# Three merge-gate chunks as block products in a Griffin-style residual block, on one Trainium2 core

## The chip, the cores and the metric

The kernel runs on one core of a Trainium2 chip. The metric is the device time of one execution in microseconds; the time of a version is the median of its runs. PE is the matrix engine (TensorE), DVE the vector engine, ACT the scalar engine, POOL GpSimd and SP the engine that issues most DMAs. Products of PE land in PSUM, which has eight banks; a tile of 128 x 512 fp32 fills one.

## What is computed

One layer on 512 frames of 1024 features, fp32:

```python
xn = rmsnorm(x, norm_mix_g)
q, k, v, xr, gr, ga, gb = split(xn @ w_in)                 # seven blocks of 1024 columns
ya = chunked_band_attention(q, k, v, rel_table) @ w_attn_out
xc = causal_depthwise_conv(xr, conv_w, conv_b)
hr = rg_lru(xc, ...)                                        # gates r, i; a scan over the frames
yb = (hr * gelu(gr)) @ w_rnn_out
g_a, g_b = sigmoid(ga + b_a), sigmoid(gb + b_b)             # the merge gates
h = x + (g_a * ya + g_b * yb) @ w_o
h = h + (silu(hn @ Wg) * (hn @ Wu)) @ w_ffn_out             # hn = rmsnorm(h)
out = rmsnorm(h, final_norm_g)
```

## The kernel before

**Arithmetic.** Every fp32 operand of PE is split into a high part (ACT copies it into fp32r) and a low part (DVE subtracts), and each product is three matmuls: high by high, high by low, low by high (`mm3`, L74 to L78; `split`, L80 to L83).

**Chunks.** The weights come in chunks of 256 columns (two tiles of 128) by 1024 rows. Their order is the list `chunks` (`plan`, L96, and the loops behind it). `prefetch(n)` (L308) loads and splits chunks in that order up to number n; `weights(name, ahead)` (L336) does so for a chunk and `ahead` more. A load is two DMAs of 512 KB from SP into `raw` tiles (three buffers); the split goes into `whl` tiles (four buffers, two for a chunk). A plain chunk is two calls of `project` (L342): for each of the two column tiles 8 blocks of rows by 3 matmuls, 512 columns wide, so 48 matmuls.

**Block products.** From chunk 2 on the two FFN input projections use seven products of blocks in place of eight: `weight_sums` (L181) makes four sums of weight blocks on DVE and splits seven blocks; `block_product` (L362) runs seven `product`s of 4 x 3 matmuls, 256 columns wide, so 84 matmuls, and lets ACT copy partial results out of PSUM between them (`keep`, L369). The other side needs four sums of blocks of the activations, made once.

**Order of the first part.** Chunks in sets by j = 0, 2, 4, 6: `xr` (conv), `gr` (GELU), `ga` for j < 4, `gb`. `gates_of(j)` (L754) is the recurrence of two channel tiles: products `rg` on PE (L709), then a chain over ACT and DVE (L721 tanh, L728 tanh, L729 exp, L731, L735, L759 square root, L740, L741 scan, L742) and the split of its result into `rnn` (L746 on ACT, L747 on POOL). Merge gates are `gate(w, j)` (L778): a projection and a tanh into `za` or `zb`. Behind the sets come q and k of head pair 0 (L858), v of the first head group (L964) and the way out of the branch, `yb` (L967 to L972): eight projections whose inner dimension is all eight `rnn` tiles, each multiplied into its gate. `scores(0)` stands ahead of the seventh. Then comes attention in a PE order written by hand (L973).

**PSUM.** Tag `mm` has four banks, `s` and `t` two each (L71). The first column tiles of `xr0` and `gr0` are begun early and hold all four `mm` banks; `rg` of j takes two `s` banks, of j + 1 two `mm` banks (L755); the first two tiles of `ga` take `t` (L779).

**What sets the order.** The tile framework's planner orders each engine's instructions by a simulated timeline: among those whose inputs and buffers are ready it takes what stands first in the program. Inside `manual_schedule` blocks the named engines keep the program's order. One such block holds ACT and DVE for the first two tiles (L785 to L800):

```python
        g = [gelu_in(0, po[0])]
        xch.append(conv_out(1, xc[1]))
        g.append(gelu_in(1, po[1]))
        prefetch(index["gb0"] + 1)
        for c in range(2):
            gelu_out(g[c], po[c])
```

`gelu_in` is L691 and L692, `gelu_out` L696 (ACT) and L697 (DVE); L697 is the last reader of the PSUM tile of `gr0`.

Of the kernel before, what the change touches and what calls it, by code (L numbers as in the profile page):

```python
# [8 lines left out]
F32 = mybir.dt.float32  # L9
# [5 lines left out]
P = 128  # L15
D = 1024
S = 512
# [21 lines left out]
def block_kernel(ctx: ExitStack, tc: tile.TileContext, x, norm_mix_g, w_in, b_merge, rel_table,  # L39
# [51 lines left out]

    chunks = []
    index = {}
    strassen = [f"f{w}{j}" for j in range(2, FT, 2) for w in "gu"]

    def plan(name, *parts, rows=0, kts=KT):  # L96
        index[name] = len(chunks)
        chunks.append((name, parts, rows, kts))

    for j in range(0, KT, 2):  # L100
# [6 lines left out]
    def plan_qk(pr):  # L107
        plan(f"qk{pr}", cols(w_in, C_Q + pr * P, P), cols(w_in, C_K + pr * P, P))
# [48 lines left out]
    def load(name, k):  # L157
        _, parts, rows, kts = chunks[index[name]]
        wide = sum(width for *_, width in parts)
        n = min(4 * CW // wide, kts - k)  # L160
        at = rows + k * P
        pl, bufs = wp, 3
        if name in strassen and name[0] == "f":
            loads[0] += 1
            pl, bufs = (room[0], 1) if loads[0] % 4 == 0 and loads[0] > 4 else (wp, 3)
        raw = pl.tile([P, n, wide], F32, tag="raw", bufs=bufs, name=f"raw_{name}_{k}")
        to = 0
        for src, col, width in parts:
            sp.dma_start(out=raw[:, :, to:to + width],
                         in_=src[at:at + n * P, col:col + width].rearrange("(k p) e -> p k e", p=P))  # L170
            to += width
        raws[name, k] = raw

    slots, loads = [0], [0]
    barrier = ["wo1"]
    room = [None]

    begun = {}
    spare = [None]

    def weight_sums(name, ahead=False):  # L181

        def blocks_of():
            for k in (0, 4):
                if (name, k) not in raws:
                    load(name, k)
            r0, r1 = raws.pop((name, 0)), raws.pop((name, 4))
            return r0[:, :, 0:P], r0[:, :, P:CW], r1[:, :, 0:P], r1[:, :, P:CW]

        if name not in begun:  # L190
            a11, a21, a12, a22 = blocks_of()
            s21, s34 = (sums_room.tile([P, 2, 4, P], F32, tag=tag, bufs=1, name=f"{tag}_{name}")
                        for tag in ("s21", "s34"))
            s2, s1, s3, s4 = s21[:, 0], s21[:, 1], s34[:, 0], s34[:, 1]
            first_sum = dve.tensor_add(s1, a21, a22)
            if name == "fu2":

                tc.keep_in_program_order(first_sum)
            dve.tensor_sub(s2, s1, a11)
            dve.tensor_sub(s3, a11, a21)  # L200
            dve.tensor_sub(s4, a12, s2)
        if ahead:
            slots[0] += 1
            o = sums_room.tile([P, 2, 2, 4, P], F32R, tag="whl", bufs=1, name=f"whl_{name}_s2")
            split(o[:, :, 0], o[:, :, 1], s21[:])
            begun[name] = (s34, {"s2": o[:, 0], "s1": o[:, 1]})
            return
        sc = room[0]
        blocks_ = {}
        if name in begun:  # L210

            a11, a21, a12, a22 = blocks_of()
            s34, blocks_ = begun.pop(name)
            s1 = s2 = None
            s3, s4 = s34[:, 0], s34[:, 1]
        for group in ((("a11", a11), ("a12", a12)), (("s2", s2), ("s1", s1)), (("s3", s3), ("s4", s4)), (("a22", a22),)):
            if group[0][0] in blocks_:
                continue
            if name == "fg2" and group[0][0][0] == "a":

                for key, src in group:
                    o = spare[0].tile([P, 2, 4, P], F32R, tag="act", bufs=13, name=f"whl_{name}_{key}")
                    split(o[:, 0], o[:, 1], src)
                    blocks_[key] = o
                continue
            pl, tag, bufs = sc, "a22", 2
            if len(group) == 2:
                slots[0] += 1
                pl, tag, bufs = (sums_room, "whl", 1) if slots[0] % 5 == 1 else (wp, "whl", 4)
# [238 lines left out]
    _, xnT = features(xnp, "xn", "xnT")  # L468


    vc = cp.tile([P, NV], F32, name="vc")
# [267 lines left out]
    def rnn_scan(j, u, a, ti, g):  # L739
        dve.scalar_tensor_tensor(ti[:], ti[:], 0.5, u, ALU.mult, ALU.mult)  # L740
        dve.tensor_tensor_scan(u, a[:], ti[:], 0.0, ALU.mult, ALU.add)  # L741
        dve.scalar_tensor_tensor(u, u, 0.5, g[:], ALU.mult, ALU.mult)  # L742
# [3 lines left out]
        act.activation(o[:, 0], u, AF.Copy)  # L746
        pool.tensor_sub(o[:, 1], u, f(o[:, 0]))  # L747
        return o

    rnn = []  # L750
# [50 lines left out]
    for j in range(0, KT, 2):  # L801
        if j:
            for c in range(2):
                conv[j + c] = rnn_conv(j + c, tile_of(f"xr{j}", c, ahead=2))
        for c in range(2):
            if j:
                po = tile_of(f"gr{j}", c, "t")
                conv[j + c] += (rnn_gelu(j + c, po),)
        if j:
            gates_of(j)  # L810
        for w in range(j // 4, 2):
            for c in range(2):
                gate(w, j + c)
            if j == w == 0:
                gates_of(j)


    def blocks(ap):
        return ap.rearrange("p (b i) -> p b i", i=P)
# [35 lines left out]
            pool.tensor_copy(kl[other, e], kl[own, e])  # L855
        qk[pr] += [kh, kl]

    q_tile(0)  # L858
    k_tile(0)
    rw2_stack.close()  # L860
    rw_stack.close()
    aw2_stack, aw2 = opened("aw2", 2)
    aw_stack, aw = opened("aw", 2, "right")

# [102 lines left out]
    for j in range(KT):  # L967
        if j == 6:
            prob = scores(0)
        po = mm_tile(f"po_yb{j}")  # L970
        project(po, weights(f"yb{j - j % 2}"), j % 2, rnn)
        dve.scalar_tensor_tensor(zB[j], zB[j], 1.0, po[:], ALU.add, ALU.mult)  # L972
# [29 lines left out]

    hp = ctx.enter_context(pool_of("h", 1, "right"))

    sums_room = ctx.enter_context(pool_of("sums", 1, "right"))
# [112 lines left out]
    def split_act(i):  # L1118
        o = act2[i]

        if i == 0:
            hi = acp.tile([P, 2, S], F32R, tag="act", bufs=13, name=f"act_hi{i}")
        elif i < 3:
            hi = sums_room.tile([P, 2, S], F32R, tag=("s21", "s34")[i - 1], bufs=1, name=f"act_hi{i}")
        else:
            if i == 3:
                hi_room.append(sums_room.tile([P, 2, 2, S], F32R, tag="whl", bufs=1, name="act_hi34"))
# [232 lines left out]
```

## Time and profile before

| | |
|---|---|
| time, median of 3 runs | 867.3 us (867.19 to 867.31) |
| the profiled execution | 867.3 us, of which 865.5 us are its span, from first to last instruction |
| PE clock granted | 0.998 of full speed |
| PE, DVE, ACT, POOL busy | 99%, 69%, 58%, 11% of the span |

A row of the page or of a view names line, engine, operation and tiles (`out<-in`). In a timeline the first two numbers are start and duration in us, xN is a count, and the bracket is the idle time of that engine just before and what ended it. A view of stretches gives the busy time of each engine in each stretch, in brackets the instructions that reach into it. Matmuls overlap in time, so the time of a stream of them is read from their starts, not from single durations.

### The profile page before, as it was taken

The page shows a single profiled execution, that of the slowest core. Times are in us where ns is not written, and L with a number is a line of the kernel's source. Part 1 is how long each engine was busy: PE and PEld are TensorE (multiplying, and loading weights), DVE is VectorE, ACT ScalarE, POOL GpSimd, SP SyncE. Part 2 cuts the span into 40 slices and gives each one's busy share as a digit, 9 for nine tenths or more (in the row PEclk, how much of TensorE's full clock was granted, in tenths as well). Part 3 has the DMA queues.
Part 4 walks back from the last instruction along what each step waited for, and adds up shares of the span by engine and source line. Part 5 has one row for each costly group of instructions (what it writes and reads, how often), then busy time and mean ns, then how long its engine had stood idle before and what let it go on. Part 6 is the DMA issues. An engine that isn't in the chain of part 4 may idle for free.

```text
span 865.5 us, 13353 instructions
## 1 busy us (share of the span) xinstructions
PE 856.4 (99%) x5130; PEld 761.1 (88%) x5130; DVE 600.9 (69%) x950; ACT 498.1 (58%) x878; POOL 95.2 (11%) x161
## 2 busy tenths in 40 slices
PE   9999999999999999999999999999999999999997
PEld 6988888888889889898888889999999999888885
DVE  5666656573456585766556556988888888698885
ACT  6595747752356585767633357555555556545434
POOL 2412111120112132221200000000000001000000
PEclk9999999999999999999999999999999999999999
DMA  9133232433323332232223712424333332437542
GB/s 289 57 119 106 68 120 76 123 98 98 109 88 95 81 103 74 81 113 64 74 76 121 266 51 72 145 79 131 109 98 98 99 98 85 148 100 227 185 134 97
DMA packets 88767, 96.39 MB, mean 111 GB/s; under 512 B 5784, under 2 KB 74992, under 8 KB 88704
## 3 DMA queue, kind: packets, MB, share of 16 engines
q1 hardware_dynamic: 87072, 92.03, 34.3%
q10 hardware_dynamic: 1232, 2.95, 0.9%
q8 instruction: 40, 0.66, 0.3%
q0 software_dynamic: 400, 0.57, 0.2%
q14 instruction: 23, 0.19, 0.1%
HBM read 93.39 MB, written 2.14 MB: 110 GB/s over the span
## 4 chain that ended last, share of the span: by engine, by line
PE 97%; DVE 1%; ACT 1%; DMA 0%; issue 0%; ACTq 0%; DVEq 0%
PE po_out L76 2%; PE po_out L77 2%; PE po_out L78 2%; PE o L941 2%; PE p_fu L78 2%; PE p_fg L78 2%; PE p_fg L77 2%; PE p_fg L76 2%; PE p_fu L76 2%; PE p_fu L77 2%; PE pT L921 2%; PE po_v L76 2%; PE po_v L78 2%; PE po_v L77 2%; PE po_gb L76 2%; PE po_xr L77 2%
## 5 line engine op out<-in xcount | busy, mean ns | idle before, releaser
L910 POOL TENSOR_SCALAR p<-p,rl 128x128 f32<-128x128 f32 (+3 forms) x61 | 34.9, 590 | 135.7 <-DVE rl L906 135.4
L905 ACT ACTIVATE p<-p,m 128x128 f32<-128x128 f32 (+1 forms) x64 | 35.7, 560 | 11.0 <-DVE m L904 10.8
L76 PE MATMUL po_v<-whl_v,xnT 128*128 128x256 f32 x128 | 36.5, 285 | 0.0
L78 PE MATMUL po_v<-whl_v,xnT 128*128 128x256 f32 x128 | 36.2, 283 | 0.0
L77 PE MATMUL po_v<-whl_v,xnT 128*128 128x256 f32 x128 | 36.2, 283 | 0.0
L1131 POOL TENSOR_TENSOR act_lo<-act,act_hi 128x1024 fp32r<-128x1024 f32 x1 | 2.4, 2405 | 300.7 <-ACT act_hi L1130 300.7
L76 PE MATMUL po_out<-whl_fo,act_hi 128*128 128x512 f32 (+1 forms) x80 | 30.8, 385 | 0.5 <-ACT c_u L370 0.5
L78 PE MATMUL po_out<-whl_fo,act_lo 128*128 128x512 f32 (+1 forms) x80 | 30.7, 384 | 0.0
L77 PE MATMUL po_out<-whl_fo,act_hi 128*128 128x512 f32 (+1 forms) x80 | 30.7, 384 | 0.0
L904 DVE CUSTOM_DVE_ANT_0 p<-s,bias 128x128 f32<-128x128 f32 (+1 forms) x64 | 29.1, 483 | 1.0 <-PE s L896 1.0
L83 DVE TENSOR_TENSOR whl_qk<-raw_qk,whl_qk 128x1024 fp32r<-128x1024 f32 x16 | 20.5, 1284 | 13.2 <-ACT whl_qk L82 13.0
L83 DVE TENSOR_TENSOR whl_fu_s<-s_fu,whl_fu_s 128x1024 fp32r<-128x1024 f32 x20 | 24.1, 1222 | 6.2 <-ACT whl_fu_s L82 6.2
L77 PE MATMUL po_xr<-xnT,whl_xr 128*128 128x512 f32 (+1 forms) x80 | 27.7, 353 | 0.0
L83 DVE TENSOR_TENSOR pp<-pT,pp 128x384 fp32r<-128x384 f32 (+1 forms) x48 | 27.5, 596 | 0.1
L77 PE MATMUL po_gr<-xnT,whl_gr 128*128 128x512 f32 (+1 forms) x80 | 27.5, 347 | 0.0
L78 PE MATMUL po_gr<-xnT,whl_gr 128*128 128x512 f32 (+1 forms) x80 | 27.3, 347 | 0.0
L78 PE MATMUL po_xr<-xnT,whl_xr 128*128 128x512 f32 (+1 forms) x80 | 27.2, 346 | 0.0
L76 PE MATMUL po_gr<-xnT,whl_gr 128*128 128x512 f32 (+1 forms) x80 | 27.2, 347 | 0.0
L83 DVE TENSOR_TENSOR whl_fg_s<-s_fg,whl_fg_s 128x1024 fp32r<-128x1024 f32 x20 | 24.0, 1222 | 4.1 <-ACT whl_fg_s L82 4.0
L76 PE MATMUL po_xr<-xnT,whl_xr 128*128 128x512 f32 (+1 forms) x80 | 26.3, 351 | 0.4 <-ACT xnT L566 0.4
L82 ACT ACTIVATE whl_qk<-raw_qk 128x1024 fp32r<-128x1024 f32 x16 | 16.8, 1053 | 17.0 <-PE po_yb L78 10.4
L76 PE MATMUL po_gb<-xnT,whl_gb 128*128 128x512 f32 x64 | 25.2, 394 | 0.0
(487 smaller groups left out, 3247.5 us busy)
## 6 DMA issues: line engine op xcount, KB each, us to landing
raw_fg<-in_w_ffn_in_dram SPq DMA_DIRECT2D x24, 512.0 KB, 4.2
raw_fu<-in_w_ffn_in_dram SPq DMA_DIRECT2D x22, 512.0 KB, 3.9
raw_qk<-in_w_in_dram SPq DMA_DIRECT2D x32, 256.0 KB, 3.2
raw_fo<-in_w_ffn_out_dram SPq DMA_DIRECT2D x16, 512.0 KB, 3.6
raw_xr<-in_w_in_dram SPq DMA_DIRECT2D x8, 512.0 KB, 4.3
raw_gr<-in_w_in_dram SPq DMA_DIRECT2D x8, 512.0 KB, 3.6
raw_ga<-in_w_in_dram SPq DMA_DIRECT2D x8, 512.0 KB, 4.7
raw_gb<-in_w_in_dram SPq DMA_DIRECT2D x8, 512.0 KB, 3.5
```

What stands on the lines that cost most here:

```text
L76: pe.matmul(o, sh, mh, start=start, stop=False, skip_group_check=parts)
L77: pe.matmul(o, sh, ml, start=False, stop=False, skip_group_check=parts)
L78: pe.matmul(o, sl, mh, start=False, stop=stop, skip_group_check=parts)
L82: act.activation(hi, src, AF.Copy)
L83: dve.tensor_sub(lo, src, f(hi))
L904: dve.tensor_tensor_reduce(prob[qb][:], scs[qb][:, 0:w], bias[:, S - w:S], -1.0, 3e38, ALU.add, ALU.min, nmax[:, qb:qb + 1])
L905: act.activation(prob[qb][:], prob[qb][:], AF.Exp, bias=nmax[:, qb:qb + 1], scale=-1.0, accum_out=lsum[:, qb:qb + 1])
L910: eng.tensor_scalar(prob[qb][:], prob[qb][:], rl[:, qb:qb + 1], 1.0, ALU.mult, ALU.mult)
L921: pe.transpose(pt[:, at * P:(at + 1) * P], prob[qb][:, kb * P:(kb + 1) * P], ident[:])
L941: pe.matmul(po[:, S - n:S], st, pp[i][:, part, lo:lo + n], start=kb == 0 and part == 0, stop=kb == NT - 1 and part == 1)
L1131: (dve if i else pool).tensor_sub(lo[:], o[:], f(hi[:]))
```

## The change

- The chunk list gets a new order: xr0 gr0 ga0 **gb6** xr2 gr2 ga2 xr4 gr4 **qk0** xr6 gr6 **yb0 yb2 yb4 gb0 gb2 gb4 yb6 v0**, and then as before. So gb6 and ga0 stand behind the first pair, q and k of pair 0 between the third and the fourth set.
- gb0, gb2 and gb4 are computed as block products, with weight sums and four sums of blocks of `xnT`. Those sums are eight DVE operations of 1024 elements on each partition, four of them pinned behind the set j = 2, four behind the first GELU of the set j = 6. They lie in gate tiles that are not yet in use.
- Behind the recurrence: the splits of the four sums, the way out for yb0, yb2 and yb4 (ACT copies the result to `zb`), the three block gates (tanh, then one DVE operation that multiplies gate and way out), and the last two way-out tiles as before. Then `scores(0)`, and behind it v of the first group.
- The buffers for it are a new pool `gs`, where the recurrence's pool was.
- The low part of `rnn` 6 and 7 goes from POOL to DVE.
- The prefetch in the block quoted above goes one chunk further, up to xr2.

```diff
-    strassen = [f"f{w}{j}" for j in range(2, FT, 2) for w in "gu"]
+    strassen = ["gb0", "gb2", "gb4"] + [f"f{w}{j}" for j in range(2, FT, 2) for w in "gu"]
...
     for j in range(0, KT, 2):
         plan(f"xr{j}", cols(w_in, C_XR + j * P))
         plan(f"gr{j}", cols(w_in, C_GR + j * P))
         if j < 4:
             plan(f"ga{j}", cols(w_in, C_GA + j * P))
-        plan(f"gb{j}", cols(w_in, C_GB + j * P))
+        if j == 0:
+            plan("gb6", cols(w_in, C_GB + 6 * P))
+        if j == 4:
+            plan_qk(0)
...
-    plan_qk(0)
+    for name in ("yb0", "yb2", "yb4", "gb0", "gb2", "gb4", "yb6"):
+        plan(name, cols(*((w_in, C_GB + int(name[2]) * P) if name[0] == "g" else (w_rnn_out, int(name[2]) * P))))
     plan_v(0)
-    for j in range(0, KT, 2):
-        plan(f"yb{j}", cols(w_rnn_out, j * P))
...
-        pool.tensor_sub(o[:, 1], u, f(o[:, 0]))
+        (pool if j < 6 else dve).tensor_sub(o[:, 1], u, f(o[:, 0]))
...
-        prefetch(index["gb0"] + 1)
+        prefetch(index["xr2"] + 1)
...
+    def sums_of_x():
+        homes = [zs[w][j][:].rearrange("p a (b n) -> p (a b) n", n=256) for w, j in ((0, 2), (0, 3), (1, 2), (1, 1), (1, 0))]
+        x12, x22, t1, t2, t3 = homes
+        t4 = x12
+        todo = (lambda: dve.tensor_add(x12, f(block_of_x(0, 1, 0)), f(block_of_x(0, 1, 1))),
...
+        for n, what in enumerate(todo):
+            tc.keep_in_program_order(what())
+            if n == 3:
+                yield
+        yield t1, t2, t3, t4
+
+    for j in range(0, KT, 2):
+        if j:
+            for c in range(2):
+                conv[j + c] = rnn_conv(j + c, tile_of(f"xr{j}", c, ahead=2))
+            for c in range(2):
+                po = tile_of(f"gr{j}", c, "t")
+                conv[j + c] += (rnn_gelu(j + c, po),)
+                if j + c == 6:
+                    x_sums = next(sums_)
+            gates_of(j)
+        if j < 4:
+            for c in range(2):
+                gate(0, j + c)
+        elif j == 4:
+            q_tile(0)
+            k_tile(0)
+        if j == 0:
+            gates_of(0)
+            for c in range(2):
+                gate(1, 6 + c)
+        if j == 2:
+            sums_ = sums_of_x()
+            next(sums_)
...
+    def way_out(j):
+        for c in range(2):
+            po = mm_tile(f"po_yb{j + c}")
+            project(po, weights(f"yb{j}"), c, rnn)
+            act.activation(zB[j + c], po[:], AF.Copy)
+
+    def block_gate(j, n, x_right):
+        z, o = zs[0][2 + n % 2], zs[1][j // 2]
+        block_product(f"gb{j}", n % 2, x_right, z[:].rearrange("p a (b n) -> p (a b) n", n=256))
+        for c in range(2):
+            at = 24 + j + c
+            act.activation(z[:, c], z[:, c], AF.Tanh, bias=hb[:, at:at + 1], scale=0.5)
+        dve.scalar_tensor_tensor(o[:], z[:], 1.0, o[:], ALU.add, ALU.mult)
+
+    for i in (3, 2, 1, 4):
+        split_pair(bt_homes[i], x_sums[i - 1])
...
+    for j in (0, 2, 4):
+        way_out(j)
+    for n, j in enumerate((0, 2, 4)):
+        block_gate(j, n, x_right)
+
+    for j in (6, 7):
+        po = mm_tile(f"po_yb{j}")
+        project(po, weights("yb6"), j % 2, rnn)
+        dve.scalar_tensor_tensor(zB[j], zB[j], 1.0, po[:], ALU.add, ALU.mult)
...
-        po = mm_tile(f"po_v{gr}_{t}", "mm" if gr else "t")
+        po = mm_tile(f"po_v{gr}_{t}", "mm" if gr or t > 1 else "t")
...
+    prob = scores(0)
     for t in range(NT):
         v_tile(0, t)
```

More of the change, by code (lines that the diff above doesn't have):

```diff
@@ L162, in load @@
         pl, bufs = wp, 3
-        if name in strassen and name[0] == "f":
+        if name in strassen:
             loads[0] += 1
@@ L176, in block_kernel @@
     room = [None]
+    sums_room = [None]
     begun = {}
@@ L203, in weight_sums @@
             slots[0] += 1
-            o = sums_room.tile([P, 2, 2, 4, P], F32R, tag="whl", bufs=1, name=f"whl_{name}_s2")
+            o = sums_room[0].tile([P, 2, 2, 4, P], F32R, tag="whl", bufs=1, name=f"whl_{name}_s2")
             split(o[:, :, 0], o[:, :, 1], s21[:])
@@ L467, in block_kernel @@
     gm = cp.tile([P, 8], F32, name="gm")
-    _, xnT = features(xnp, "xn", "xnT")
+    xnT_all, xnT = features(xnp, "xn", "xnT")
     vc = cp.tile([P, NV], F32, name="vc")
@@ L800, in block_kernel @@
             conv[c] = xc[c], xch[c], g[c]
[L801 to L815, printed above, removed]
     def blocks(ap):
@@ L856, in k_tile, with block_of_x @@
         qk[pr] += [kh, kl]
-    q_tile(0)
-    k_tile(0)
+    def block_of_x(kh, half, part):
+        return xnT_all[:, 4 * kh:4 * kh + 4, part, half * 256:half * 256 + 256]
+    def sums_of_x():
[3 more added lines that the diff above has]
+        todo = (lambda: dve.tensor_add(x12, f(block_of_x(0, 1, 0)), f(block_of_x(0, 1, 1))),
+                lambda: dve.tensor_sub(t1, x12, f(block_of_x(0, 0, 0))),
+                lambda: dve.tensor_sub(t1, t1, f(block_of_x(0, 0, 1))),
+                lambda: dve.tensor_add(x22, f(block_of_x(1, 1, 0)), f(block_of_x(1, 1, 1))),
+                lambda: dve.tensor_sub(t2, x22, t1),
+                lambda: dve.tensor_sub(t3, x22, x12),
+                lambda: dve.tensor_sub(t4, f(block_of_x(1, 0, 0)), t2),
+                lambda: dve.tensor_add(t4, t4, f(block_of_x(1, 0, 1))))
+        for n, what in enumerate(todo):
[3 more added lines that the diff above has]
+        yield t1, t2, t3, t4
@@ L860, in block_kernel @@
     rw2_stack.close()
     rw_stack.close()
+    gs_stack, gs = opened("gs")
+    bt_homes = {i: gs.tile([P, 2, 4, 256], F32R, name=f"xt{i}") for i in (2, 1, 3, 4)}
+    sums_room[0] = room[0] = gs
+    def way_out(j):
[10 more added lines that the diff above has]
+        dve.scalar_tensor_tensor(o[:], z[:], 1.0, o[:], ALU.add, ALU.mult)
@@ new lines, in block_kernel @@
+    for i in (3, 2, 1, 4):
+        split_pair(bt_homes[i], x_sums[i - 1])
+    x_right = right_side(lambda kh, half, part, k: block_of_x(kh, half, part)[:, k], [bt_homes[i] for i in range(1, 5)])
+    for j in (0, 2, 4):
[6 more added lines that the diff above has]
+        dve.scalar_tensor_tensor(zB[j], zB[j], 1.0, po[:], ALU.add, ALU.mult)
@@ L862, in block_kernel @@
+    gs_stack.close()
     aw2_stack, aw2 = opened("aw2", 2)
@@ L962, in laid @@
                 3: ([qs(second)], [ks(second)])}[at]
+    prob = scores(0)
     for t in range(NT):
         v_tile(0, t)
[L967 to L972, printed above, removed]
     with tc.manual_schedule(engines={mybir.EngineType.PE}):
@@ L1003, in block_kernel @@
     hp = ctx.enter_context(pool_of("h", 1, "right"))
-    sums_room = ctx.enter_context(pool_of("sums", 1, "right"))
+    sums_room[0] = ctx.enter_context(pool_of("sums", 1, "right"))
+    slots[0] = loads[0] = 0
     hn_stack, hnp = opened("hnT", 1, "right")
```

12 lines of the change are left out of this document (6 added, 6 removed).

## The prediction

> **What bounds the kernel now.** I read the page first: the busy row and the chain that ended last.
>
> ```profile
> span 865.5 us, 13353 instructions
> PE 856.4 (99%) x5130; PEld 761.1 (88%) x5130; DVE 600.9 (69%) x950; ACT 498.1 (58%) x878; POOL 95.2 (11%) x161
> PE 97%; DVE 1%; ACT 1%; DMA 0%; issue 0%; ACTq 0%; DVEq 0%
> ```
>
> PE is busy 99% of the span and is 97% of the chain. Whether it is also without holes is told by the list of PE's waits, which has four rows:
>
> ```profile
> PE busy L396 <- DVE eps_t L402: 1.2, 1, 1.2
> PE pt_mix_0t L564 <- DVE xs_mix L544: 0.6, 2, 0.4
> PE po_out L76 <- ACT c_u L370: 0.5, 1, 0.5
> PE po_xr L76 <- ACT xnT L566: 0.4, 2, 0.2
> ```
>
> These are 2.7 us in all, and none lies between the first projections and the end of the FFN's input. So a change there wins only what it takes from the stream of matmuls, and loses every microsecond for which PE has nothing ready. For the price of the stream I took two stretches: one whole plain gate chunk (48 matmuls of 512 columns), and a piece of the FFN with block products alone (matmuls of 256 columns).
>
> ```profile
> core 0: us, PE busy (x), PEclk, DMA share, GB/s
> 94.57:105.45 10.88, 10.88 (x50) 1.00 0.32 97
> 570.00:670.80 100.80, 100.80 (x842) 1.00 0.34 105
> ```
>
> Two of the matmuls of each row only reach in over the edge. 10.88 / 48 is 0.2267 us for a wide matmul, 100.80 / 840 is 0.1200 us for a narrow one.
>
> **The saving.** A plain chunk costs 48 x 0.2267 = 10.88 us, a block chunk 84 x 0.1200 = 10.08 us. That is 0.80 us for a chunk and **2.40 us** for three. The numbers of matmuls are fixed by the code, and nothing else leaves PE: 864.9 us is the floor.
>
> [...]
>
> **What the block form asks of the other engines.** A block chunk adds on DVE four weight sums, the low parts of seven blocks, two additions from PSUM, and here one multiplication of 1024 elements; on ACT five copies out of PSUM. The FFN runs exactly this without a hole:
>
> ```profile
> core 0: us, PE busy (x) PEld busy (x) DVE busy (x) ACT busy (x) POOL busy (x), PEclk, DMA share, GB/s
> 560.00:740.00 180.00, 180.00 (x1503) 180.00 (x1502) 146.57 (x201) 107.16 (x191) 2.40 (x1) 1.00 0.34 105
> L1146 DVE TENSOR_TENSOR act<-act,c_u 128x1024 f32<-128x1024 f32 x9 | 11.0, 1219 | 0.3 <-ACT c_u L370 0.3
> ```
>
> DVE is 81% busy there and ACT 60%, so three such chunks in a row cost PE nothing once the first one's operands are there; without that cover a chunk's DVE work would take 146.57 / 180 x 10.08 = 8.2 us. The first operands have the three way-out chunks (32.6 us of PE) ahead of them. The eight sums of x are 1.22 us each (row above), 4.9 us in each batch. The first batch lies under the rest of set 2 and xr4. The second is pinned behind the GELU of tile 6, runs under the products of gr7, and ends near the end of the last gate products; the next 9 us of the chain there are nearly all ACT's. I cost both at nothing. The loads are as many and as large, on the same queue. Six way-out results are copied by ACT (0.63 us) where DVE multiplied (0.69 us); two low parts go from POOL to DVE. These shorten the chain or are neutral. `scores(0)` had 10.9 us of way-out tiles behind it and now has the 96 narrow matmuls of v, 11.5 us: nothing.
>
> **First new wait: the bank that gb6 needs (+2.5 us).** The prefetch in the hand-ordered block now takes in both splits of xr2, ahead of both `gelu_out`. Before, the planner put these splits between and behind them:
>
> ```profile
> 41.81 0.63 ACT L679 ACTIVATE xch<-xc 128x512 fp32r<-128x512 f32 x1 [4.47 <-DVE xc L675]
> 42.35 0.58 ACT L691 ACTIVATE g<-po_gr 128x512 f32<-128x512 f32 x1
> 42.83 2.00 ACT L82 ACTIVATE whl_gb<-raw_gb 128x1024 fp32r<-128x1024 f32 x2
> 44.72 0.62 ACT L696 ACTIVATE g<-g 128x512 f32<-128x512 f32 x1
> 48.64 1.06 ACT L82 ACTIVATE whl_xr<-raw_xr 128x1024 fp32r<-128x1024 f32 x1 [0.32 <-DMA raw_xr<-in_w_in_dram]
> 43.91 2.36 DVE L83 TENSOR_TENSOR whl_gb<-raw_gb,whl_gb 128x1024 fp32r<-128x1024 f32 x2 [0.26 <-ACT whl_gb L82]
> 46.19 0.68 DVE L697 SCALAR_TENSOR_TENSOR g<-g,po_gr 128x512 f32<-128x512 f32 x1
> 47.92 0.68 DVE L697 SCALAR_TENSOR_TENSOR g<-g,po_gr 128x512 f32<-128x512 f32 x1
> 49.73 1.23 DVE L83 TENSOR_TENSOR whl_xr<-raw_xr,whl_xr 128x1024 fp32r<-128x1024 f32 x1 [1.12 <-ACT whl_xr L82]
> 47.52 1.66 PE L709 MATMUL rg<-xch,wrg 64*128 64x512 f32 x12
> 49.11 0.50 PE L76 MATMUL po_gb<-xnT,whl_gb 128*128 128x512 f32 x1
> 18.74 18.91 SPq L169 DMA_DIRECT2D raw_gb<-in_w_in_dram  x2
> 39.52 6.01 SPq L169 DMA_DIRECT2D raw_xr<-in_w_in_dram  x2
> DMA to landing us min/median/max: 3.5/3.5/3.6
> ```
>
> First, the block's order is strict: ACT sat idle 4.47 us up to 41.81 although the gate chunk's first half was on its way since 18.74 and its split waited for none of what came in between. Second, the second half of xr2 cannot come sooner: its load goes out at 45.2 (the end of row 39.52, less 0.37 us of issue), when the first low part of the gate chunk has freed one of three raw buffers, and lands 3.5 us later, at 48.6. Now put that split ahead of `gelu_out`: high part until 49.7, low part until 50.96, then the first L697, which ends at 51.6 instead of 46.87. L697 is the last reader of a `gr0` tile. Of the four `mm` banks two hold the `gr0` tiles and two the gate products of tile 1, just finished; gb6 is next on PE at 49.11 and needs one of them. PE waits until 51.6: **2.5 us**. Behind it nothing is ready: xr2 needs the same banks, gr2's weights have not been loaded. Lower bound 0, if a bank comes free otherwise; upper bound 6.2, if the eight L721 (5.6 us) also go ahead of the tanh and the banks come with those, at 55.3. I take 2.5, where each term has its row.
>
> **Second new wait: the way out behind the recurrence (+1.0 us).** In the kernel before 35 us of gb6, q, k and v (163.34 to 198.34) stood between the last gate products and `yb`. Now `yb` follows at once, and each of its tiles needs `rnn` 6 and 7 for the last 6 of 24 matmuls. Four `mm` banks let PE do 4 x 18 x 0.2267 = 16.3 us ahead of them; that the planner does fill holes so is seen at 190.98, where seven `yb` matmuls stand between those of v. One block product of gb0 needs no `mm` bank (12 x 0.12 = 1.4 us), so the cover is 17.8 us. The chain before:
>
> ```profile
> 161.75 1.66 PE L709 MATMUL rg<-xch,wrg 64*128 64x512 f32 x12
> 163.34 0.50 PE L76 MATMUL po_gb<-xnT,whl_gb 128*128 128x512 f32 x1
> 171.59 0.66 ACT L780 ACTIVATE zb<-po_gb,hb 128x512 f32<-128x512 f32 x1
> 174.26 1.63 DVE L83 TENSOR_TENSOR whl_v<-raw_v,whl_v 128x1024 fp32r<-128x1024 f32 x1
> 175.13 1.05 ACT L82 ACTIVATE whl_v<-raw_v 128x1024 fp32r<-128x1024 f32 x1
> 176.20 1.28 ACT L759 ACT_TABLE_LOAD   x1
> 182.81 1.17 ACT L746 ACTIVATE rnn<-u 128x512 fp32r<-128x512 f32 x2 [2.23 <-DVE u L742]
> 190.98 0.40 PE L76 MATMUL po_yb<-rnn,whl_yb 128*128 128x512 f32 x1
> 198.34 0.40 PE L77 MATMUL po_yb<-rnn,whl_yb 128*128 128x512 f32 x1
> ```
>
> From 163.34 to the end of the first of the two copies (182.81 and half of 1.17) are 20.1 us. Of these 0.66 go with the gate that is no longer there, and the splits of v (1.63 and 1.05) were in the way too; without all three it is 16.8. Now the splits of yb and gb0 stand in their place, in part. I take 18.8 us, between, so PE waits **1.0 us**. Bounds: 0, and 3.8 (20.1 against 16.3 without the block product). The evictions behind it also wait for the split of the third sum of x, but 5.4 us of matmuls of the four open tiles remain, which cover ACT's 1.05, DVE's 1.22 and the copy.
>
> **The sum.** 867.3 - 2.4 + 2.5 + 1.0 = **868.4 us**. The profiled execution took 867.3 us (1.8 us outside the span), the same as the median.
>
> **The rivals.** I count as a difference what is over 0.2%, 1.73 us, about what a measurement of this kernel can tell from no change. So faster means stalls under 0.67 us in all, slower means over 4.13.
>
> Rival A, gb6 finds a bank: then 867.3 - 2.4 + 0 to 1.0, **864.9 to 865.9 us**. For it: in the kernel before the first L697 was over 2.2 us ahead of need, and the planner may sort gb6 ahead of tile 1's gate products. Against it: those products are ready first, and the four banks are counted out. Chance 0.24, of which 0.20 is under 865.57.
>
> Rival B, the recurrence is late: from 19.4 us after the gate products on (cover and 1.63 us), the way out alone pushes the sum over the bound; at 20.1 without the block product the time is 867.3 - 2.4 + 2.5 + 3.8 = **871.2 us**. For it: before it was 20.1, and both engines get more to do. Against it: the chain's own work is nearer 17. Chance 0.32.
>
> Rival C, narrow matmuls are slower in the new place: in the FFN the weight loads (PEld) are busy all 180 us, so nothing is left there; one load takes
>
> ```profile
> L76 PEld LDWEIGHTS po_ga<-xnT,whl_ga x16: 187/188/192, 36.0 to 46.5; 128*128 128x128 f32 x16
> ```
>
> 0.188 us, and were they not overlapped, three chunks would take 3 x (84 x 0.188 - 10.88) = 14.7 us more, **882 us**. Loads overlap wherever this trace has such products: chance 0.01. [...]
>
> The forecast itself has 0.43, from 867 to 869. So **faster 0.20**, **same 0.47** (0.43 and 0.04 of A), **slower 0.33**. The range 864.9 to 870.9 goes from the floor to nearly rival B's end and leaves out about one in ten.
>
> **What would show it.** Saving: three stretches of 84 narrow matmuls at 0.120 us ahead of attention, and wide ones unchanged. First wait: PE's list of waits gets a row for `po_gb` released by L697 on DVE, some 2.5 us near 49; if gb6 starts at 49.1, the step is wrong. Second wait: a row for `po_yb` released by `rnn`, 0 to 3.8 us, near 172 (163.34 less the chunk that has left, 10.9, and with the first wait, 2.5, and the cover). Block gates: no PE idle in them; waits for `keep` copies (L370) or `whl_gb` there would say that DVE or ACT is the bound. Wrong altogether would be a gain over 2.4 us, or stalls in attention or the FFN, whose code is as before.

## The result and the profile after

The changed kernel takes **875.56 us** (median of five, 874.20 to 876.00), the kernel before beside it 867.19 us: a ratio of 1.0091, 95% interval 1.0077 to 1.0106. It is slower by 8.4 us, where 1.1 us had been forecast. The profiled execution took 874.2 us.

The page of the changed kernel: span, busy row and chain.

```profile
span 872.4 us, 13641 instructions
PE 857.0 (98%) x5238; PEld 765.9 (88%) x5238; DVE 630.6 (72%) x988; ACT 515.3 (59%) x912; POOL 95.4 (11%) x159
PE 89%; DVE 4%; ACT 4%; DMA 1%; issue 1%; POOL 0%; ACTq 0%; DVEq 0%
```

DVE and ACT have 8% of the chain between them, where they had 2%: PE now waits for them. The list of PE's waits says where (the lines of the gates and the recurrence lie 3 further down, so L697 is L700, L721 is L724, L735 is L738, L746 is L749, L759 is L762):

```profile
PE po_yb L76 <- ACT rnn L749: 4.0, 1, 4.0
PE po_gb L76 <- DVE g L700: 2.7, 1, 2.7
```

These are the two rows that the prediction named, and the only new ones. The rest shows in the view of stretches, here of PE alone: length, busy time with matmuls, granted clock, DMA share, GB/s.

```profile
core 0: us, PE busy (x), PEclk, DMA share, GB/s
154.80:171.30 16.50, 16.50 (x74) 1.00 0.28 83
171.30:175.40 4.10, 0.17 (x1) 0.76 0.14 50
175.40:180.20 4.80, 4.73 (x11) 0.50 0.38 112
194.80:204.80 10.00, 10.00 (x85) 1.00 0.46 135
```

The first row is the way out ahead of the recurrence's last tiles: four banks, 16.4 us from first start to the end of the last. The second is the wait. The third was in no plan: **the granted clock is 0.50**, and 11 matmuls take 4.84 us from start to start, 0.43 us each after the first, in place of 11 x 0.2267 = 2.49. The fourth is a stretch of the block gates at 0.12 us a matmul, without a hole. (The list gives the second wait as 4.0 us; from the end of the matmul before, by the distance of the starts, to the next start are 4.1.)

The sum for the profiled execution: -2.4 (block form) + 2.7 (first wait) + 4.1 (second wait) + 2.3 (matmuls at half clock, 4.84 - 2.49) = 6.7 us, of the 6.9 us by which the span grew. The term of 2.3 us is what the matmuls lost there; the section on the prediction shows that a late copy would have cost as much at full clock. Three of the five executions took some 1.5 us more; the first experiment bears on that.

### The profile page after: what moved, and what is told of

Read it like the earlier page. It is cut to its first block, busy times and chain, and to the rows that moved or that the text cites. A ratio compares the mean times of both kernels' runs of the same rounds, so it can differ in the third digit from the quotient of the medians.

```text
span 872.4 us, 13641 instructions
## 1 busy us (share of the span) xinstructions
PE 857.0 (98%) x5238; PEld 765.9 (88%) x5238; DVE 630.6 (72%) x988; ACT 515.3 (59%) x912; POOL 95.4 (11%) x159
## 4 chain that ended last, share of the span: by engine, by line
PE 89%; DVE 4%; ACT 4%; DMA 1%; issue 1%; POOL 0%; ACTq 0%; DVEq 0%
PE po_out L76 2%; PE po_out L78 2%; PE po_out L77 2%; PE o L1008 2%; PE p_fu L78 2%; PE p_fg L78 2%; PE p_fg L77 2%; PE p_fg L76 2%; PE p_fu L76 2%; PE p_fu L77 2%; PE pT L988 2%; PE po_v L76 2%; PE po_v L78 2%; PE po_v L77 2%; PE po_ya L76 2%; PE po_h L76 2%
## 5 line engine op out<-in xcount | busy, mean ns | idle before, releaser
L76 PE MATMUL po_yb<-rnn,whl_yb 128*128 128x512 f32 x64 | 26.2, 418 | 4.0 <-ACT rnn L749 4.0
L83 DVE TENSOR_TENSOR whl_qk<-raw_qk,whl_qk 128x1024 fp32r<-128x1024 f32 x16 | 21.8, 1364 | 11.0 <-ACT whl_qk L82 10.7
L77 PE MATMUL po_yb<-rnn,whl_yb 128*128 128x512 f32 x64 | 25.6, 401 | 0.0
```

What stands on the lines that cost most here:

```text
L76: pe.matmul(o, sh, mh, start=start, stop=False, skip_group_check=parts)
L77: pe.matmul(o, sh, ml, start=False, stop=False, skip_group_check=parts)
L83: dve.tensor_sub(lo, src, f(hi))
```

## The experiments

Twelve kernels. Theory: the loss is the two waits, and what a wait does to PE's clock; the block form brings its 2.4 us. Rivals: a wait is not the prefetch's (or not the cover's) doing; the sums of x on DVE delay the recurrence; the half clock has another cause than the wait; the saving is not there.

**One line of the change alone.** The kernel before, with only the deeper prefetch:

```diff
-        prefetch(index["gb0"] + 1)
+        prefetch(index["xr2"] + 1)
```

> The kernel before with one line of the change alone: the prefetch in the hand-ordered block goes on to xr2. Theory (the split of xr2 ahead of both gelu_out holds a PSUM bank that the next gate chunk needs): PE waits 2.7 us for L697 near 49 us, as it does in the changed kernel, and the time is 867.2 + 2.7 = 869.9 us. Rival (that wait is made up later, by work that it lets come sooner, or stands only beside the other changes): 867.2 us.

871.30 us (869.71, 871.27, 871.32, 871.34), ratio 1.0043 (1.0028 to 1.0058). PE's longest wait in this kernel:

```profile
PE po_gb L76 <- DVE g L697: 2.6, 1, 2.6
```

and the stretch behind it, of PE alone:

```profile
51.60:55.00 3.40, 3.40 (x8) 0.50 0.49 157
```

The wait is the predicted one, in size and place (2.5 had been worked out). But three of four executions take 1.6 us more than that explains, and the profiled one of these has PE at half clock for 3.41 us behind the wait: 8 matmuls, where the changed kernel's profiled execution has 15 in the same 3.4 us at full clock. The mean granted clock of each execution sorts them alike: 0.999 in the run of 869.71, 0.997 in the three others.

**The pause filled.** The same kernel, with ten matmuls of 512 columns that nobody reads, between the gate products and gb6's place in the order (here gb0), in a spare bank:

```diff
+                for n in range(10):
+                    tc.keep_in_program_order(pe.matmul(warm_p[:], xnT[0][:, 0, 0:P], xnT[0][:, 0], start=True, stop=True))
```

> The kernel of b1_prefetch_further with ten matmuls of 512 that nobody reads put between the gate products of set 0 and those of gb0, in a spare bank: they fill 2.3 us of the 2.6 us in which TensorE waits for its first bank there. The chain of the bank is left as it was, so the wait's price of 2.5 us stays. If the half clock comes from TensorE's pause: no execution has the dip, all lie at 867.2 + 2.5 = 869.7 us, where b1 had 871.3 in three of four. Rival: the dip has another cause (the load of the other engines, a time of its own), it stays at 51.6 us or comes elsewhere, and the median stays at 871.3 us.

869.89 us (869.60 to 870.15, six runs), ratio 1.0031 (1.0019 to 1.0043). In this kernel the stretch of the wait and the one behind it read

```profile
48.00:51.60 3.60, 3.60 (x20) 1.00 0.87 286
51.60:55.00 3.40, 3.00 (x14) 1.00 0.58 170
```

The chain of the bank is as it was, and 0.4 us of the wait is left behind the fillers. The profile has no half clock, the mean clock of the six executions is 0.998 or 0.999, and all lie within 0.5 us of the one execution of the kernel above that had none. So the wait's own price is 2.8 us, and **the half clock is caused by PE's pause and costs 1.4 us more here**.

**The prefetch as it was.** The changed kernel with `prefetch(index["gb6"] + 1)` in the block.

> The changed kernel with the prefetch one chunk shorter, up to gb6. Theory: the wait of 2.7 us near 49 us goes and nothing else changes: 874.2 to 876.0 less 2.7, so 871.5 to 873.3 us; the wait for rnn and the half clock behind it stay. Rival (the prefetch of xr2 was needed elsewhere): as slow as the change, or slower.

871.53 us (871.47 to 871.71), ratio 1.0051 (1.0034 to 1.0067): 4.0 us less than the change. The first wait is gone, `po_yb` still waits 4.0 us, and the half clock behind it is as long (a mean clock of 0.75 from 168 to 175 us and of 0.77 from 175 to 182 make some 6.7 us of it; in the changed kernel it lasts from 173.44 to 180.27). As expected: the first wait and its clock are this one line's doing, and the rest of the loss lies at the recurrence.

**More cover behind the recurrence, by q and k.** The changed kernel, with q and k of pair 0 behind the gate products of set 6 in place of set 4, in the chunk list and in the loop.

```diff
-        if j == 4:
+        if j == 6:
             plan_qk(0)
...
-        elif j == 4:
+        elif j == 6:
             q_tile(0)
```

> The changed kernel with q and k of head pair 0 (10.9 us of PE) moved from behind set 4 to behind the gate products of set 6, so that they lie between these and the way out. Theory (PE runs out of work while the recurrence ends, and the 4.2 us without matmuls halve the clock for the matmuls behind): wait and half clock both go, 4.2 and 2.6 us: 874.2 - 6.8 = 867.4 us, and the runs lie closer together than 874.2 to 876.0. Rival (DVE and ACT are late with sums and splits whatever stands there): the wait moves behind q and k, and 2 us or more of it stay: over 869 us.

871.99 us (871.87 to 872.20), ratio 1.0055 (1.0040 to 1.0070). PE's two longest waits:

```profile
PE po_gb L76 <- DVE g L700: 2.8, 1, 2.8
PE po_yb L76 <- ACT rnn L749: 2.0, 1, 2.0
```

The rival's outcome came, over 869 us with 2.0 us of the wait left. PE has a chunk of 10.9 us more to do there, but the wait shrinks by 2.0 only. The view that groups ACT's instructions between 150 and 176 us shows a good part of why:

```profile
L841 ACT ACTIVATE kh<-po_k 64x512 fp32r<-64x512 f32 x2 | 1.2, 594 | 1.9 <-DVE kl L840 1.9
```

This and its like are q's and k's way out of PSUM (busy time, mean ns of one, idle time ahead of it and its cause); they hold ACT and DVE while the chain of the recurrence needs them. The first copy of `rnn` starts 24.5 us after the gate products, where it was 19.9 in the changed kernel. Of these 4.6 us, 1.3 lie ahead of the chain's first tanh, where nothing of q or k has run yet; from that tanh to the copy are 21.8 us in place of 18.5. Cover that needs the engines of the chain lengthens the chain. That they are late whatever stands there, the rival's reason, is what the cover by gb6 below refutes.

**Both.** The two edits above together.

> Both of the edits: prefetch one chunk shorter, q and k behind the gate products of set 6. Theory: only the saving of the block products is left, 867.2 - 2.4 = 864.8 us, up to 865.5 if moving q and k makes a small wait of its own. Rival (block products cost as much as plain ones here): 867.2 us or more.

869.10 us, ratio 1.0021 (1.0012 to 1.0031): one execution at 867.58 with a mean clock of 0.999, nine from 868.96 to 869.36 at 0.996 and 0.997. Missed by 3.6 us: the wait of 2.0 us stays, and in nine of ten executions the half clock comes with it.

**More cover, by gb6.** The changed kernel with gb6 behind the gate products of set 6, and q and k where the change has them.

```diff
-        if j == 0:
+        if j == 6:
             plan("gb6", cols(w_in, C_GB + 6 * P))
...
             gates_of(0)
+        if j == 6:
             for c in range(2):
                 gate(1, 6 + c)
```

> The changed kernel with the light chunk gb6 moved from behind the first pair to behind the gate products of set 6, ahead of the way out; q and k stay behind set 4, the prefetch line stays (xr2 is now the chunk behind ga0, so it loads as many chunks as the kernel before did). Theory: gb6 is 10.9 us of matmuls with one tanh a tile behind it, and unlike q and k it gives ACT and DVE little to do. Cover 10.9 + 16.3 = 27.2 us against some 20.6 us of recurrence, so the wait for rnn goes altogether; the bank wait near 49 us goes too, since xr2 stands where gb0 stood. Left is the saving: 867.1 - 2.4 = 864.7 us, runs close together. Rival (DVE and ACT are late whatever the cover, as with q and k): a wait for rnn of 1 us or more stays, 866 us or more. Rival 2 (with one light chunk less behind the first pair the chain of set 0 is late for set 2): a new wait between 50 and 110 us.

867.88 us, ratio 1.0009 (1.0000 to 1.0017). Both waits are gone: gb6 asks for one tanh a tile behind its products, the recurrence keeps its pace (its first copy of `rnn` ends 20.8 us after the gate products) and PE has 10.9 us more to do. A new wait stands where gb6 was taken away:

```profile
PE rg L712 <- ACT xch L682: 1.7, 1, 1.7
```

The timeline of DVE ahead of it, at 66 to 72 us:

```profile
66.29 2.77 DVE L744 TENSOR_TENSOR_SCAN u<-a,gt 128x512 f32<-128x512 f32 x2
...
70.83 0.73 DVE L678 SCALAR_TENSOR_TENSOR xc<-po_xr,vc,xc 128x509 f32<-128x509 f32 x1
```

The scans of set 0, which nobody needs soon, stand ahead of the conv's last tap, for which the gate products wait. Five executions lie at 867.06 to 867.40, five at 868.54 to 868.85, one between. The profiled one is of the slower five and has the half clock behind this wait; the mean clock of all five is 0.996, of the others 0.997 or 0.998. The second rival, a new wait between 50 and 110 us, came true.

**The scans later.** One more edit: the last three operations of set 0's recurrence (L743 to L745) are put behind the conv of set 2, and pinned there.

```diff
+        if j:
+            scans()
+
+    def scans():
         while held:
...
+            if j == 2:
+                scans()
```

> The kernel with gb6 as cover (867.1 to 868.9 us, one wait left: the gate products of set 2 wait 1.7 us for xch of tile 3, whose conv steps the planner put between the scans of set 0), with the last steps of the recurrence of set 0 (L740 of the kernel before and behind it) traced and pinned behind the conv of set 2. Theory: the conv of tile 3 ends some 4 us sooner, the wait goes, no pause of PE is left that could halve the clock, and only the saving is left: 867.1 - 2.4 = 864.7 us, 865.2 at most, with runs within 0.3 us. Rival (the scans, put off, are late for someone else): a new wait, 866 us or more.

**865.59 us**, ratio 0.9984 (0.9974 to 0.9993): faster than the kernel before (ten of eleven executions from 865.41 to 866.15; one took 1714.3 us and is left out). That is 0.4 us over the 865.2 that had been allowed. One new wait is left, and in the profile no half clock from the first projections to the end of the matmuls (mean clock 0.999):

```profile
PE rg L712 <- POOL xch L683: 0.6, 1, 0.6
```

A stretch of 10 us out of its block gates, PE alone:

```profile
190.00:200.00 10.00, 10.00 (x85) 1.00 0.35 122
```

**The saving by itself.** The last kernel, with gb0, gb2 and gb4 as plain chunks; the sums of x and their splits are still made, though nothing reads them.

```diff
-        block_product(f"gb{j}", n % 2, x_right, z[:].rearrange("p a (b n) -> p (a b) n", n=256))
...
+            po = tile_of(f"gb{j}", c)
+            act.activation(z[:, c], po[:], AF.Tanh, bias=hb[:, at:at + 1], scale=0.5)
```

> The same kernel with gb0, gb2 and gb4 at the same place as plain products (48 wide matmuls for a chunk), the sums of x and their splits kept though nobody reads them: what the block form alone is worth. Theory: 3 x (10.88 - 10.08) = 2.4 us slower than the one with block products, 867.1 us, as the kernel before. Rival (block products save less in this place, by waits for copies out of PSUM or for weight sums): under 1.5 us of difference.

868.03 us (867.84 to 868.23), beside the 865.59 on the same chip: the block form is worth **2.44 us**, 2.40 had been worked out. (The 867.1 that had been expected was missed because the kernel with block products itself lies 0.9 us over its forecast.) The same stretch holds 46 wide matmuls here, where the row above has 85 narrow ones:

```profile
190.00:200.00 10.00, 10.00 (x46) 1.00 0.34 107
```

**The last 0.6 us.** The low part of the conv's tile 7 on DVE in place of POOL.

```diff
-        pool.tensor_sub(xch[:, 1], xc[:], f(xch[:, 0]))
+        (dve if j == 7 else pool).tensor_sub(xch[:, 1], xc[:], f(xch[:, 0]))
```

> The kernel of e9_scans_later with one more edit: the low part of xch tile 7 is made on VectorE and not on GpSimd. In e9 TensorE waits 0.6 us at 140.8 us for that low part. If GpSimd is the late one: the wait is gone, 865.6 - 0.6 = 865.0 us. Rival: VectorE is as late there, the wait stays or moves to VectorE's name, 865.6 us or more.

865.62 us (ten of eleven runs from 865.48 to 865.81), ratio 0.9984 (0.9975 to 0.9993): nothing won. The wait at 140.8 us is gone, but another has come, as the rival had it in part:

```profile
PE po_yb L76 <- ACT rnn L751: 0.4, 1, 0.4
```

The recurrence ends no sooner: the first copy of `rnn` starts at 163.92 us, 163.82 in the kernel before this edit, and PE begins the matmuls that need it at 164.60 and 164.54. So the wait of 0.6 us had been hidden by this later limit, and the cover by gb6 is just long enough.

**The clock kept up at the second pause.** The kernel with the old prefetch, with 16 matmuls that nobody reads in the second wait, and the high-part products of `rnn` 6 and 7 of four tiles ahead of their low-part products.

```diff
+    for n in range(16):
+        tc.keep_in_program_order(pe.matmul(warm_p[:], pos[0][1](0, 0, slice(0, P)), rnn[0][:, 0], start=True, stop=True))
```

> The changed kernel with the shorter prefetch (871.5 us), and 16 matmuls of 512 columns into a spare bank, whose result nobody reads, pinned between the last way-out matmul that can run and the first that needs rnn 6; the products with the low parts of rnn are traced behind those with the high parts. Theory (of the 6.8 us lost there 4.2 are the wait and 2.4 to 2.6 the half clock that follows a pause of PE): the wait is filled with 3.6 us of useless work, the clock stays at 1.0, and 2.4 to 2.6 us come back: 869.0 us, with the way out as late as before. Rival (the matmuls behind the wait are slow for another reason, the low parts of rnn or the operands' place): 871.5 us, and matmuls at 0.43 us again.

871.30 us (870.45, 870.58, 872.01, 872.16), ratio 1.0048 (1.0034 to 1.0061). The two lower ones, one of them profiled, have a mean clock of 0.998, and the profile has no half clock; the others have 0.996. So with a full clock this kernel takes 870.5 us, 1.0 less than the 871.5 of the kernel with the old prefetch, where 869.0 had been expected. In the profile other waits take the place of the slow matmuls:

```profile
PE q_gb L76 <- ACT whl_gb_a L82: 1.1, 1, 1.1
PE po_yb L76 <- ACT zb L937: 0.5, 1, 0.5
```

The first is for the weights of the block gate, the second for a bank that ACT has not yet copied out. And the 1.0 us is not the clock's. The edit also moved a split of yb on DVE away from between the two L738, and the first copy of `rnn` starts at 171.06 us, 172.10 in the kernel with the old prefetch. From that copy to the first matmul of the fifth way-out tile are 9.05 us here at full clock (180.11) and 9.02 there with the half clock (181.12). So at the second pause the half clock costs nothing on top. (What makes the two upper executions 1.6 us slower is not shown: neither was profiled.)

**The sums of x earlier.** The kernel with the old prefetch, and all eight sums behind set 2.

```diff
-                if j + c == 6:
-                    x_sums = next(sums_)
...
             next(sums_)
+            x_sums = next(sums_)
```

> The changed kernel with the shorter prefetch (871.5 us) and all eight sums of x behind set 2, none behind the GELU of tile 6. If the second batch of sums (4.9 us of DVE between 2 us before and 6 us after the last gate products) makes the chain late, rnn 6 comes 1 to 2 us sooner and the time is 869.5 to 870.5. Theory (the chain's first 9 us there are ACT's, so the sums lie beside it): rnn 6 comes within 0.4 us of where it came, 871.1 to 871.6 us.

872.07 us (871.94 to 872.20), ratio 1.0057 (1.0043 to 1.0070). It is 0.5 us slower than with the sums where the change has them, and the wait for `rnn` is 4.4 us in place of 4.0. That is 0.5 us over the range that had been given for no effect, and slower, not 1 to 2 us faster: the sums do not make the recurrence late.

**The low parts on POOL.** The kernel with the old prefetch, and the low parts of `rnn` 6 and 7 back on POOL.

```diff
-        (pool if j < 6 else dve).tensor_sub(o[:, 1], u, f(o[:, 0]))
+        pool.tensor_sub(o[:, 1], u, f(o[:, 0]))
```

> The changed kernel with the shorter prefetch (871.5 us) and the low parts of rnn 6 and 7 on POOL again. Theory: the high parts set the end of the wait, and 16 matmuls need only these; a low part on POOL is 1.3 us in place of 0.65 but need not wait for the splits on DVE: the same within 0.4 us, 871.1 to 871.9. Rival (the low parts are what the way out waits for): 1 us slower or more.

875.62 us (875.51 to 875.70), ratio 1.0098 (1.0082 to 1.0113): 4.1 us slower than with them on DVE, where the same within 0.4 us had been expected; the rival was right. Behind the old wait stands a second one, and a third for the bank:

```profile
PE po_yb L76 <- ACT rnn L749: 4.0, 1, 4.0
PE po_yb L77 <- POOL rnn L750: 2.7, 1, 2.7
PE po_yb L76 <- ACT zb L903: 1.2, 1, 1.2
```

So that part of the change is needed.

## Why the prediction was wrong

**Saving, right.** 2.40 us worked out, 2.44 measured by doing and not doing it. The block gates run without PE idle time, so their sums, low parts and copies cost PE nothing while they run, as said; what is made for them ahead of that does, as the second failed step shows.

**First new wait, right in mechanism and size, short of its consequence.** The row is there, 2.7 us for 2.5, and the timeline of the changed kernel has the steps as they were worked out (ACT's lines first, then DVE's):

```profile
48.48 1.06 ACT L82 ACTIVATE whl_xr<-raw_xr 128x1024 fp32r<-128x1024 f32 x1 [2.43 <-DMA raw_xr<-in_w_in_dram]
49.44 1.13 ACT L699 ACTIVATE g<-g 128x512 f32<-128x512 f32 x2
...
49.56 1.23 DVE L83 TENSOR_TENSOR whl_xr<-raw_xr,whl_xr 128x1024 fp32r<-128x1024 f32 x1 [2.47 <-ACT whl_xr L82]
50.71 1.27 DVE L700 SCALAR_TENSOR_TENSOR g<-g,po_gr 128x512 f32<-128x512 f32 x2
```

The split of the second half ends at 50.8, the first L700 half of 1.27 later, and gb6 starts at 51.53. What the sum lacked is that PE then runs at half clock in most executions, 1.4 us more (in three of four of the kernel with this line alone; by their times in three of five of the changed one). Rival A (a bank comes free) is refuted.

**Second new wait: the failed step.** The prediction put it at 1.0 us, "cover" 17.8 against a chain of 18.8. It was 4.1. Both terms were off, as the timeline of the changed kernel shows (ACT's lines, then DVE's):

```profile
155.32 1.05 ACT L82 ACTIVATE whl_yb<-raw_yb 128x1024 fp32r<-128x1024 f32 x1
156.27 5.62 ACT L724 ACTIVATE gt<-rg,hb 64x512 f32<-64x512 f32 x8
169.48 1.06 ACT L762 ACTIVATE u<-u 128x1024 f32<-128x1024 f32 x1 [1.84 <-DVE u L738]
174.79 1.17 ACT L749 ACTIVATE rnn<-u 128x512 fp32r<-128x512 f32 x2 [3.30 <-DVE u L745]
...
167.63 1.21 DVE L83 TENSOR_TENSOR whl_yb<-raw_yb,whl_yb 128x1024 fp32r<-128x1024 f32 x1
168.76 0.68 DVE L738 SCALAR_TENSOR_TENSOR u<-u 128x512 f32<-128x512 f32 x1
```

The chain took 20.5 us, from 154.86 (the end of the gate products) to the end of the first `rnn` copy (174.79 and half of 1.17). The splits of yb took the places of the ones that had gone, in full and not "in part": one on ACT ahead of the eight tanh, one on DVE between the two L738 for which the square root waits (where this split is moved away, in the kernel that keeps the clock up, the copy of `rnn` comes 1.0 us sooner). The prediction had all rows for 20.1 and took 18.8 on the hope that some of it would go. And the block product of gb0 that was to lengthen the cover by 1.4 us did not come: its weights' first high part is made at 181.53 (a row of `whl_gb_a` below), 10 us too late. So the cover was 16.4 us, and 20.5 - 16.4 = 4.1. Rival B had this mechanism and nearly this size (3.8), at a chance of 0.32.

**The second failed step: the evictions behind it.** The prediction let 5.4 us of matmuls of the four open tiles cover the way out of the first bank, and put the step at nothing. In the changed kernel ACT waits 1.77 us for the low part of `rnn` (L750) and copies that bank out only after the splits of the sums and three of gb0's splits, which it makes without idle time between them; the last line is PE's first matmul of the fifth tile, which needs the bank:

```profile
177.73 2.95 ACT L82 ACTIVATE xt<-zb 128x1024 fp32r<-128x1024 f32 x3 [1.77 <-DVE rnn L750]
180.59 1.04 ACT L82 ACTIVATE xt<-za 128x1024 fp32r<-128x1024 f32 x1
181.53 1.66 ACT L82 ACTIVATE whl_gb_a<-raw_gb 128x512 fp32r<-128x512 f32 x3
183.10 1.06 ACT L903 ACTIVATE zb<-po_yb 128x512 f32<-128x512 f32 x2
183.72 0.50 PE L76 MATMUL po_yb<-rnn,whl_yb 128*128 128x512 f32 x1
```

From PE's restart at 175.47 to 183.72 are 8.25 us, for 24 wide matmuls and 2 narrow ones, 5.7 us at full clock: 2.6 us lost. The half clock makes the matmuls 2.3 us longer, but they only fill the time until the copy. The kernel with the sums earlier shows it. Its half clock ends at 176.76, after half as long, and from its restart at 173.21 to the fifth tile are 8.26 us all the same, now with a wait for the bank:

```profile
173.35:176.76 3.41, 3.41 (x9) 0.50 0.38 117
181.47 0.50 PE L76 MATMUL po_yb<-rnn,whl_yb 128*128 128x512 f32 x1 [0.49 <-ACT zb L902]
```

The kernel that keeps the clock up says the same (9.05 us against 9.02 from the copy of `rnn` on). No run here makes the copy earlier and changes nothing else.

**The term that was missing: the half clock.** Nothing in the prediction priced what a pause does to the matmuls behind it. At the first pause it costs 1.4 us, in most executions; at the second, as just shown, nothing on top of the late copy. (With q and k as cover and the old prefetch PE does not wait for that copy, and there the nine executions with the lower mean clock take 1.5 us more than the one without.) With the two waits at their true size and nothing else the time would have been 867.2 - 2.4 + 2.7 + 4.1 = 871.6 us, near rival B's 871.2. The 2.6 us of the late copy make it some 874.2, as two executions have it, and the half clock at the first pause 875.6 (the other three: 875.56 to 876.00), past the range's end at 870.9.

**Costs put at nothing.** The sums of x: confirmed, their place changes 0.5 us, and the change has the better one. The low parts on DVE: confirmed, and worth 4.1 us. `scores(0)` ahead of v and the loads: no wait of PE names them in the changed kernel. The copies out of PSUM are the step above. Rival C (narrow matmuls slower) is refuted by the rows at 0.12 us.

So where did the gain go? It was not lost: 2.4 us came in full, but the two waits took 6.8 us, the late copy 2.6, and in three of five executions the half clock at the first pause some 1.4 more. With gb6 as the cover of the last recurrence, where it also needs no bank at 49 us, and the scans out of the conv's way, the same block form gives 865.6 us.

## What to carry to other kernels

On a path that PE bounds, a pause can cost more than its length (the first one here 2.8 us, and 1.4 more in most executions): ask of each new wait (here from 1.7 us on) what the clock does behind it, and add that as a term of its own, but not where another wait behind the pause takes the same time anyway. Ask also what stands on the copying engine's list ahead of the copy that frees a bank. When work is taken out from under a chain, time the chain from the rows as they are, and assume that what is moved in its place stands in the same spots of the same engines. Cover a chain with work that asks little of the chain's engines: gb6 with its one tanh a tile did it, q and k with their splits did not.

## What the hardware showed

**Half clock behind a pause of PE.** In the changed kernel's trace the granted clock is 0.50 from 173.44 to 180.27 us, 6.83 us long. In the kernel with the prefetch line alone it is 0.50 from 51.58 to 54.99, in the one with gb6 as cover (before the scans were moved) from 75.19 to 78.60, in the one with the sums earlier from 173.35 to 176.76: 3.41 us each, half of 6.83. So PE's work is read here in stretches of that length, counted from where the clock falls. The changed kernel, the one with the prefetch line alone, the one with gb6 as cover and the one with the low parts on POOL, each with the clock in the last column but two:

```profile
47.15:50.56 3.41, 1.73 (x13) 1.00 0.97 314
50.56:53.97 3.41, 2.44 (x11) 1.00 0.72 224
170.03:173.44 3.41, 1.44 (x7) 1.00 0.50 150
173.44:176.85 3.41, 1.38 (x3) 0.50 0.02 5
176.85:180.27 3.42, 3.42 (x9) 0.50 0.50 152
```

```profile
48.17:51.58 3.41, 0.85 (x8) 1.00 0.88 292
51.58:54.99 3.41, 3.39 (x8) 0.50 0.49 157
```

```profile
71.77:75.19 3.42, 1.69 (x10) 1.00 0.00 0
75.19:78.60 3.41, 3.41 (x9) 0.50 0.49 154
```

```profile
167.22:170.63 3.41, 1.73 (x8) 1.00 0.52 154
170.63:174.05 3.42, 1.09 (x4) 1.00 0.02 5
174.05:177.46 3.41, 0.68 (x2) 0.50 0.51 154
```

In each of the four the full-clock stretch just ahead of the half clock has 1.73 us or more without PE work (1.97, 2.56, 1.73 and 2.33 us). The three full-clock stretches that a full clock follows have 1.68 us or less: 1.68 twice (the first row of the first and of the last block) and 0.97. The first pause of the changed kernel's profiled execution lies in two of these stretches, 1.68 us in one and 0.97 in the next, and there the clock stayed at 1.00; the kernel with the prefetch line alone has 2.56 us in one. That the place of a pause decides whether half clock follows is the author's reading of these few rows; no run tests it.

Among the executions, sorted by time and mean clock, the kernel with a wait of 1.7 us in its profile (gb6 as cover) shows the half clock in five of eleven, the one with 2.0 us (both edits) in nine of ten, the one with 2.6 us (the prefetch line alone) in three of four.

**POOL beside a busy DVE.** In the kernel with the low parts of `rnn` 6 and 7 on POOL the two took 5.09 us:

```profile
172.99 5.09 POOL L750 TENSOR_TENSOR rnn<-u,rnn 128x512 fp32r<-128x512 f32 x2 [8.34 <-ACT rnn L749]
```

and in the kernel before 2.55 us:

```profile
183.53 2.55 POOL L747 TENSOR_TENSOR rnn<-u,rnn 128x512 fp32r<-128x512 f32 x2 [8.71 <-ACT rnn L746]
```

The view of the tile in the first of these kernels, of POOL alone, tells the two apart (least, median and greatest ns, first and last start):

```profile
L750 POOL TENSOR_TENSOR rnn<-u,rnn x2: 1267/2564/3861, 173.0 to 176.8; 128x512 fp32r<-128x512 f32 x2
```

The first took 3.86 us, the second, from 176.8 us on, 1.27, as long as each of the two in the kernel before (1.29). DVE ran a split and three weight sums from 172.70 to 175.73 us, then nothing until 179.20. So it is the one beside the busy DVE that was slow. This is a single case: in the kernel before DVE was busy for some 1.5 of the 2.55 us, with other operations (L842 and a split of yb), and neither was slow. What makes the difference is not shown.
